# Sixteen conditioning chunks summed on VectorE and POOL, with ones-column products on TensorE, and called at other places

## The chip, the cores and the metric

The kernel runs on one core of a Trainium2 chip. The metric is the device time of one execution in microseconds (us), read as the median of several runs. Engines are named as in the profile: PE is TensorE (its weight loads are PEld), DVE is VectorE, ACT is ScalarE, POOL is GpSimd, SP is SyncE, which issues the loads.

## What is computed

The program is the forward pass of two transformer blocks in float32 on 512 tokens of width 1024. The change lies in the first block. Its conditioning vector `mx` is a product of one row with a 1024 x 6144 matrix:

```python
mx = (jax.nn.silu(c) @ w_ada[l] + b_ada[l])[:, None, :]
sh1, sc1, ga1, sh2, sc2, ga2 = jnp.split(mx, 6, axis=-1)
mc = jax.nn.silu(c_ctx) @ w_ada[l] + b_ada[l]
csh1, csc1, cga1, csh2, csc2, cga2 = jnp.split(mc, 6, axis=-1)
px = modulate(rmsnorm(x, g_norm1[l]), sh1, sc1) @ w_in[l]
x = x + ga1 * branch_merge(px, h_mx, w_fourier[l], w_mlstm[l], w_out[l])
hx2 = modulate(rmsnorm(x, g_norm2[l]), sh2, sc2)
x = x + ga2 * expert_choice(hx2, w_router[l], w_gate_e[l], w_up_e[l], w_down_e[l])
```

Of `mc`, only the first two parts are needed. Between the first and the second modulation stand the projections, a 3x3 grid convolution of q and k, a bidirectional m-LSTM, a Fourier branch and the product with `w_out`.

## The kernel before, in words

`w_ada` is worked off in 24 chunks of 256 columns. `ada_load` (L325) brings one chunk as a raw tile of 128 partitions x 8 x 256, 1 MB, by SP. `ada_sums` (L328) multiplies it on PE: for each k of 0 to 7 the stationary operand is `csil[:, k]`, 128 x 32 (column 0 is silu(c), column 1 silu(c_ctx), the rest zeros), and the moving operand the 256 columns of the chunk. Four k share one bank as four groups of 32 rows. A float32 product runs in two passes, so eight products are 16 rows of the trace. ACT copies the result to `R` (L335), and a product with `sel2`, a 128 x 2 selector, sums the four groups.

The first eight chunks are needed at the start of the block, before anything else, and are not touched. The other sixteen are put into a queue `self.bg`: chunks 12 to 19 by `ada_col` (shift and scale of the second modulation, wanted as columns: `R` is stationary, `sel2` moves; L572), then 8 to 11 and 20 to 23 by `ada_row` (the two gates, wanted as rows: `sel2` is stationary, `R` moves; L559), whose rows go through DRAM (`gad`). Each call of `pump()` (L121) takes one from the queue. It is called where a 1 MB weight tile has just been asked for: in `gemm_ws` (L146), `gemm_ta` (L173), `branch_steps` (L201) and by the k part of the q/k loop (L644). So the sixteen are worked off one by one between 100 and 440 us: four in the q/k convolution stage, two in the Fourier input product, four in the Fourier branch, two in the output gate product, four in the m-LSTM branch.

A weight tile is split before its use by `wsplit` (L125): ACT rounds it to `wH` (L129), POOL subtracts to get `wL` (L130), and PE makes three products for each k (L89, L90, L91; the last one reads `wL`). The q/k convolution (`ev_qk`, L592) is nine taps of multiply and add on DVE (L597, L608); `ctx_state` (L612) does the same for the context (`kacc`, L618 to L622). In the m-LSTM (L664 on), which alternates with the Fourier branch (`branch_steps`, made a generator `fill`), POOL scales `qd` (L682) and adds the two directions (`hs`, L730), which PE then transposes (`hT`, L735). The order on an engine is that of a scheduler, which goes by the dependencies of the program. Loads go into raw tiles that rotate, six of 1 MB at this point.

Of the kernel before, what the change touches and what calls it, by code (L numbers as in the profile page):

```python
# [8 lines left out]
F32 = mybir.dt.float32  # L9
# [3 lines left out]
OP = mybir.AluOpType  # L13
# [68 lines left out]
class Builder:  # L82
# [62 lines left out]

    def gemm_ws(self, w, c0, ncols, act, evac, ct0=0):  # L146

        for cc in range(0, ncols, 256):
            r = self.cols_chunk(w, c0 + cc, 8, 256)
            self.pump()  # L150
            for q in (0, 128):
                evac(ct0 + (cc + q) // 128, self.ws_tile(r, q, act, 8))
# [46 lines left out]
    def branch_steps(self, wb, w_in, gate_off, act, hact, new_th, evac):  # L199

        nc = self.nc  # L201
        for cc in range(0, 1024, 512):
            wr = self.raw(wb[:, cc:cc + 512].rearrange("(k p) c -> p k c", p=128), 4, 512)
            for c2 in range(0, 512, 256):
                gr = self.cols_chunk(w_in, gate_off + cc + c2, 8, 256)
                self.pump()
                for c3 in (0, 128):
                    pg = self.ws_tile(gr, c3, hact, 8)
                    th = new_th()
                    nc.scalar.activation(out=th, in_=pg, func=AF.Tanh, scale=0.5)  # L210
                    py = self.ws_tile(wr, c2 + c3, act, 4)
                    evac((cc + c2 + c3) // 128, th, py)
                    yield
# [105 lines left out]

    def ada_chunk(self, j, pool):  # L320

        return self.ada_sums(self.ada_load(j), pool)

    def ada_load(self, j):
        return self.cols_chunk(self.I["w_ada"][0], j * 256, 8, 256)  # L325

    def ada_sums(self, r, pool):
        nc = self.nc  # L328
        ps = self.pa(256, name="pada")
        for kk in range(0, 8, 4):  # L330
            for q in range(4):
                nc.tensor.matmul(ps[32 * q:32 * q + 32, :], self.csil[:, kk + q, :], r[:, kk + q, :],
                                 start=kk == 0, stop=kk == 4, tile_position=(0, 32 * q))
        R = pool.tile([128, 256], F32, tag="R", name="R")
        nc.scalar.activation(out=R, in_=ps, func=AF.Copy)  # L335
        return R

    def phase_a(self, right):
        tc, nc, I = self.tc, self.nc, self.I
# [216 lines left out]

        self.gad = gad = self.drp.tile([2, 1024], F32, name="gad")

        def ada_row(j):  # L559
            w, c = divmod(j - 8 if j < 12 else j - 16, 4)  # L560
            b = tw(n=256, name="bada")[0:1]
            nc.sync.dma_start(out=b, in_=I["b_ada"][0:1, j * 256:(j + 1) * 256])
            R = self.ada_chunk(j, sm)
            ps = self.pa(256)
            nc.tensor.matmul(ps[0:2], self.sel2, R, start=True, stop=True)
            V.tensor_tensor(b, ps[0:1], b, op=OP.add)
# [5 lines left out]
        def ada_col(j):  # L572
            R = self.ada_chunk(j, sm)
            ps = self.pa(4)
            for q in range(2):
                nc.tensor.matmul(ps[:, 2 * q:2 * q + 2], R[:, q * 128:(q + 1) * 128], self.sel2, start=True, stop=True)
            dst = (self.sh2, self.gs2)[(j - 12) // 4]
            k = 2 * (j % 4)
            c = 112 + 2 * (j - 12)
            pv = ps.rearrange("p (a b) -> p a b", b=2)[:, :, 0]  # L580
            V.tensor_tensor(dst[:, k:k + 2], pv, b1[:, c:c + 2], op=OP.add)
            if j >= 16:
# [58 lines left out]
        for c2 in (0, 256):  # L641
            self.gemm_ws(w_in, OQ + c2, 256, hx, ev_qk, c2 // 128)
            r = self.cols_chunk(w_in, OK_ + c2, 8, 256)
            self.pump()  # L644
            for q in (0, 128):
# [1436 lines left out]
```

## Time and profile before

| what | value |
|---|---|
| median of the runs | 1710.59 us (1710.18 to 1715.16, three runs) |
| the profiled execution | 1714.91 us; its span, first to last instruction, 1713.1 us |
| mean granted clock of PE | 0.969 |
| PE busy | 1579.9 us, 92% of the span |
| DVE busy | 856.2 us, 50% |
| ACT busy | 613.5 us, 36% |
| POOL busy | 564.9 us, 33% |

Durations in the rows below are from the one profiled execution. A busy share is a mean over stages that differ; the stretch that matters here is the first quarter of the span, 80 to 460 us. In a row of a timeline stand the start in us, the busy us, the engine, the line of the program, the operation, the tiles (out<-in), the shapes and how many instructions the row holds; in brackets follow idle time ahead of it and what ended it.

### The profile page before, as it was taken

The page shows a single profiled execution, that of the slowest core. Times are in us where ns is not written, and L with a number is a line of the kernel's source. Part 1 is how long each engine was busy: PE and PEld are TensorE (multiplying, and loading weights), DVE is VectorE, ACT ScalarE, POOL GpSimd, SP SyncE. Part 2 cuts the span into 40 slices and gives each one's busy share as a digit, 9 for nine tenths or more (in the row PEclk, how much of TensorE's full clock was granted, in tenths as well). Part 3 has the DMA queues.
Part 4 walks back from the last instruction along what each step waited for, and adds up shares of the span by engine and source line. Part 5 has one row for each costly group of instructions (what it writes and reads, how often), then busy time and mean ns, then how long its engine had stood idle before and what let it go on. Part 6 is the DMA issues. An engine that isn't in the chain of part 4 may idle for free. (4 is left out here: it accounts for less than half of the span.)

```text
span 1713.1 us, 20867 instructions
## 1 busy us (share of the span) xinstructions
PE 1579.9 (92%) x7702; PEld 1049.7 (61%) x7702; DVE 856.2 (50%) x1595; ACT 613.5 (36%) x1277; POOL 564.9 (33%) x447
## 2 busy tenths in 40 slices
PE   5988999999999999999999978999999989789994
PEld 3766667777776444344344337778666766566663
DVE  4388554423554122022202137997754463667776
ACT  3433354433432000000000034325763354467773
POOL 1213314344513000000000014575443342647765
PEclk9999999999999999999999988999999999889997
DMA  9522412364746999999999983322112328369944
GB/s 302 172 89 91 139 56 93 126 202 148 256 164 245 396 409 409 409 409 409 409 409 409 409 268 124 99 81 91 50 50 85 124 79 327 108 238 346 346 161 165
DMA packets 165548, 381.23 MB, mean 223 GB/s; under 512 B 16302, under 2 KB 74742, under 8 KB 165436
## 3 DMA queue, kind: packets, MB, share of 16 engines
q1 hardware_dynamic: 161116, 371.63, 59.0%
q0 software_dynamic: 4320, 8.16, 1.3%
q8 instruction: 63, 1.03, 0.3%
q14 instruction: 49, 0.40, 0.1%
HBM read 367.40 MB, written 19.93 MB: 226 GB/s over the span
## 5 line engine op out<-in xcount | busy, mean ns | idle before, releaser
L130 POOL TENSOR_TENSOR wL<-raw,wH 128x512 fp32r<-128x512 f32 x220 | 312.0, 1423 | 424.5 <-ACT wH L129 396.1
L129 ACT ACTIVATE wH<-raw 128x512 fp32r<-128x512 f32 x240 | 149.6, 628 | 256.8 <-PE ps L90 149.7
L1068 PE MATMUL ps<-raw,xT 128*64 128x512 f32 x1024 | 240.8, 595 | 0.0
L1068 PEld LDWEIGHTS ps<-raw,xT 128*64 128x64 f32 x1024 | 74.3, 137 | 137.3 <-issue 133.4
L1125 POOL TENSOR_TENSOR yL<-y,yH 128x512 fp32r<-128x512 f32 x14 | 17.9, 1278 | 419.4 <-ACT yH L1124 409.2
L1122 DVE SCALAR_TENSOR_TENSOR y<-ps,valF,ga 128x512 f32<-128x512 f32 x16 | 12.0, 751 | 228.0 <-PE ps L1068 206.8
L91 PE MATMUL ps<-raw,wL 128*128 128x512 f32 (+1 forms) x320 | 120.6, 377 | 2.9 <-POOL wL L130 2.9
L89 PE MATMUL ps<-raw,wH 128*128 128x512 f32 (+1 forms) x320 | 121.3, 379 | 0.7 <-ACT raw L188 0.7
L90 PE MATMUL ps<-raw,wH 128*128 128x512 f32 (+1 forms) x320 | 121.0, 378 | 0.0
L1316 DVE SCALAR_TENSOR_TENSOR cacc<-upad,dwc,cacc 128x512 f32<-128x512 f32 x120 | 118.0, 1036 | 0.9
L1068 PE MATMUL ps<-raw,hidT 128*64 128x512 f32 x448 | 109.3, 594 | 2.8 <-DMA raw<-in_w_down_e 2.8
L89 PE MATMUL ps<-hx,wH 128*128 128x512 f32 x224 | 91.7, 409 | 3.3 <-ACT wH L129 3.3
L91 PE MATMUL ps<-hx,wL 128*128 128x512 f32 x224 | 90.7, 405 | 2.1 <-POOL wL L130 2.1
L1882 DVE TENSOR_TENSOR wL<-raw,wH 128x512 fp32r<-128x512 f32 x96 | 88.4, 976 | 4.6 <-ACT wH L1881 3.3
L1902 POOL TENSOR_TENSOR dL<-raw,dH 128x512 fp32r<-128x512 f32 x64 | 81.6, 1295 | 27.8 <-ACT dH L1901 27.3
L90 PE MATMUL ps<-hx,wH 128*128 128x512 f32 x224 | 90.5, 404 | 0.0
L1124 ACT ACTIVATE yH<-y 128x512 fp32r<-128x512 f32 x16 | 10.0, 626 | 212.7 <-DVE y L1122 212.7
L1107 ACT ACTIVATE hidT<-pa 128x512 f32<-128x512 f32 x16 | 9.6, 597 | 205.0 <-PE pa L1106 205.0
L1068 PEld LDWEIGHTS ps<-raw,hidT 128*64 128x64 f32 x448 | 36.2, 137 | 73.5 <-issue 62.7
L91 PEld LDWEIGHTS ps<-raw,wL 128*128 128x128 f32 x320 | 61.2, 191 | 15.0 <-POOL wL L130 3.4
L89 PEld LDWEIGHTS ps<-raw,wH 128*128 128x128 f32 x320 | 61.4, 192 | 12.2 <-ACT raw L188 1.1
L90 PEld LDWEIGHTS ps<-raw,wH 128*128 128x128 f32 x320 | 61.1, 191 | 11.4 <-issue 0.5
(618 smaller groups left out, 3419.6 us busy)
## 6 DMA issues: line engine op xcount, KB each, us to landing
raw<-in_w_gate_e SPq DMA_DIRECT2D x64, 1024.0 KB
raw<-in_w_up_e SPq DMA_DIRECT2D x64, 1024.0 KB
raw<-in_w_down_e SPq DMA_DIRECT2D x64, 1024.0 KB
raw<-in_w_in SPq DMA_DIRECT2D x34, 1024.0 KB
raw<-in_w_ada SPq DMA_DIRECT2D x24, 1024.0 KB
raw<-in_expert_w_gate SPq DMA_DIRECT2D x32, 512.0 KB
raw<-in_expert_w_up SPq DMA_DIRECT2D x32, 512.0 KB
raw<-in_expert_w_down SPq DMA_DIRECT2D x16, 1024.0 KB
```

The source lines that it names most:

```text
L89: mm(ps, l[0], r[0], start=first, stop=False)
L90: mm(ps, l[0], r[1], start=False, stop=False)
L91: mm(ps, l[1], r[0], start=False, stop=last)
L129: i = self.nc.scalar.activation(out=H, in_=raw_ap, func=AF.Copy)
L130: j = (eng or self.lsub).tensor_tensor(out=L, in0=raw_ap, in1=H, op=OP.subtract)
L1068: nc.tensor.matmul(ps[o, :], act[:, k, o], r[:, q, h * 512:(h + 1) * 512], start=k == 0, stop=k == 7, tile_position=(0, 64 * i))
L1122: V.scalar_tensor_tensor(y, py[e], self.valF[:, p:p + 1], ga2[:, e, :], op0=OP.mult, op1=OP.mult)
L1124: AC.activation(out=H, in_=y, func=AF.Copy)
L1125: (nc.gpsimd if p < 7 else V).tensor_tensor(out=L, in0=y, in1=H, op=OP.subtract)
L1316: V.scalar_tensor_tensor(acc, src, c, acc, op0=OP.mult, op1=OP.add)
L1882: V.tensor_tensor(out=L3, in0=w, in1=H3, op=OP.subtract)
L1902: (nc.gpsimd, V)[DL[i]].tensor_tensor(out=L, in0=src, in1=H, op=OP.subtract)
```

## The change

A new helper `ada_parts` sums a chunk ahead of PE. DVE makes A, 128 x 256, from k = 0 to 4 (one tensor_scalar, four scalar_tensor_tensor, each with one column of `csil` as the scalar). POOL multiplies the three slices k = 5 to 7 in place in the raw tile by their columns of `csil`, broadcast along the row, in one 128 x 768 instruction, and adds the three in two more of 128 x 256. PE then sums over the partitions with a ones column: in `ada_row` two products (ones stationary, A and B moving), in `ada_col` four (A and B stationary in halves of 128 columns, the ones moving). The copy to `R` and the products with `sel2` go away for these sixteen chunks. The second change is where the queue is pumped: `gemm_ws` for q and the k part no longer do it, and `branch_steps` does it for each tile of 128 columns instead of for every two.

```diff
-    def gemm_ws(self, w, c0, ncols, act, evac, ct0=0):
+    def gemm_ws(self, w, c0, ncols, act, evac, ct0=0, pump=True):
...
-            self.pump()
+            if pump:
+                self.pump()
...
                 gr = self.cols_chunk(w_in, gate_off + cc + c2, 8, 256)
-                self.pump()
                 for c3 in (0, 128):
+                    self.pump()
...
+    def ada_parts(self, r, pool):
+
+        V, G = self.nc.vector, self.nc.gpsimd
+        A = pool.tile([128, 256], F32, tag="R", name="A")
+        V.tensor_scalar(A, r[:, 0, :], self.csil[:, 0, 0:1], None, op0=OP.mult)
+        for k in range(1, 5):
+            V.scalar_tensor_tensor(A, r[:, k, :], self.csil[:, k, 0:1], A, op0=OP.mult, op1=OP.add)
+        B = r[:, 5:8, :]
+        G.tensor_tensor(out=B, in0=B, in1=self.csil[:, 5:8, 0:1].to_broadcast([128, 3, 256]), op=OP.mult)
+        for i in (1, 2):
+            G.tensor_tensor(out=B[:, 0], in0=B[:, 0], in1=B[:, i], op=OP.add)
+        return A, B[:, 0]
...
+        ones = sm.tile([128, 1], F32, name="ones", bufs=1)
+        nc.gpsimd.memset(ones, 1.0)
...
-            R = self.ada_chunk(j, sm)
+            AB = self.ada_parts(self.ada_load(j), sm)
             ps = self.pa(256)
-            nc.tensor.matmul(ps[0:2], self.sel2, R, start=True, stop=True)
+            for i, A in enumerate(AB):
+                nc.tensor.matmul(ps[0:1], ones, A, start=i == 0, stop=i == 1)
...
-            R = self.ada_chunk(j, sm)
-            ps = self.pa(4)
+            AB = self.ada_parts(self.ada_load(j), sm)
+            ps = self.pa(2)
             for q in range(2):
-                nc.tensor.matmul(ps[:, 2 * q:2 * q + 2], R[:, q * 128:(q + 1) * 128], self.sel2, start=True, stop=True)
+                for i, A in enumerate(AB):
+                    nc.tensor.matmul(ps[:, q:q + 1], A[:, q * 128:(q + 1) * 128], ones, start=i == 0, stop=i == 1)
...
-            V.tensor_tensor(dst[:, k:k + 2], pv, b1[:, c:c + 2], op=OP.add)
+            V.tensor_tensor(dst[:, k:k + 2], ps, b1[:, c:c + 2], op=OP.add)
...
-            self.gemm_ws(w_in, OQ + c2, 256, hx, ev_qk, c2 // 128)
+            self.gemm_ws(w_in, OQ + c2, 256, hx, ev_qk, c2 // 128, False)
             r = self.cols_chunk(w_in, OK_ + c2, 8, 256)
-            self.pump()
```

The pump places are now: none in the q/k convolution, two in the Fourier input product, eight in the Fourier branch, two in the output gate product, and the first four tiles of the m-LSTM branch. The lines of the changed kernel are 13 or 14 further down: L608 becomes L622, L682 becomes L695, L730 becomes L743.

How this moves instructions is shown at three places. First POOL in the Fourier branch, around the second m-LSTM head; `wL` is the split of a weight tile, `W` the scaling of `qd`, `hs` the addition of the two directions. Before:

```order
L682 TENSOR_TENSOR W<-W,qacc 128x512
L130 TENSOR_TENSOR wL<-raw,wH 128x512 x3
L730 TENSOR_TENSOR hs<-hs,hb 128x256 x2
L682 TENSOR_TENSOR W<-W,qacc 128x512
L130 TENSOR_TENSOR wL<-raw,wH 128x512 x3
```

In the changed kernel, at the same place:

```order
L695 TENSOR_TENSOR W<-W,qacc 128x512
L130 TENSOR_TENSOR wL<-raw,wH 128x512 x3
L344 TENSOR_TENSOR raw<-raw,csil 128x768
L346 TENSOR_TENSOR raw<-raw 128x256 x2
L743 TENSOR_TENSOR hs<-hs,hb 128x256 x2
L695 TENSOR_TENSOR W<-W,qacc 128x512
L130 TENSOR_TENSOR wL<-raw,wH 128x512
L344 TENSOR_TENSOR raw<-raw,csil 128x768
L130 TENSOR_TENSOR wL<-raw,wH 128x512
L346 TENSOR_TENSOR raw<-raw 128x256 x2
L130 TENSOR_TENSOR wL<-raw,wH 128x512
```

A multiply and its two adds now stand ahead of the two `hs`, and a multiply and its adds around the next `wL`.

Second DVE in the q/k convolution, at the second k tile; `qacc` is a sum of taps, `kacc` that of the context. Before:

```order
L597 TENSOR_SCALAR qacc<-qin,cols_85 128x512
L608 SCALAR_TENSOR_TENSOR qacc<-qin,cols_85,qacc 128x7x63 x2
L608 SCALAR_TENSOR_TENSOR qacc<-qin,cols_85,qacc 128x448
L610 SCALAR_TENSOR_TENSOR qacc<-qin,qacc 128x512
L608 SCALAR_TENSOR_TENSOR qacc<-qin,cols_85,qacc 128x7x63
L618 TENSOR_SCALAR kacc<-kin,cols_85 128x256
L608 SCALAR_TENSOR_TENSOR qacc<-qin,cols_85,qacc 128x8x63
```

In the changed kernel:

```order
L611 TENSOR_SCALAR qacc<-qin,cols_85 128x512
L340 TENSOR_SCALAR A<-raw,csil 128x256
L622 SCALAR_TENSOR_TENSOR qacc<-qin,cols_85,qacc 128x7x63
L624 SCALAR_TENSOR_TENSOR qacc<-qin,qacc 128x512
L622 SCALAR_TENSOR_TENSOR qacc<-qin,cols_85,qacc 128x448
L342 SCALAR_TENSOR_TENSOR A<-raw,csil,A 128x256
L622 SCALAR_TENSOR_TENSOR qacc<-qin,cols_85,qacc 128x7x63
L632 TENSOR_SCALAR kacc<-kin,cols_85 128x256
L622 SCALAR_TENSOR_TENSOR qacc<-qin,cols_85,qacc 128x8x63
```

One chain for A is woven in between the taps; its last three links follow a few rows later.

Third PE at a row chunk of the Fourier branch; `hT` is the transposition of `hs`, the rows of L89 to L91 with `hx` are the gate product. Before:

```order
L735 MATMUL hT<-ident,hs 128x128 x4
L678 MATMUL bcM<-MS,selR 128x512
L332 MATMUL pada<-raw,csil 32x256 x8
L90 MATMUL ps<-hx,wH 128x512
L91 MATMUL ps<-hx,wL 128x512
L89 MATMUL ps<-hx,wH 128x512
L565 MATMUL pa<-R,sel_81 2x256
```

In the changed kernel:

```order
L748 MATMUL hT<-ident,hs 128x128 x4
L691 MATMUL bcM<-MS,selR 128x512
L579 MATMUL pa<-A,ones 1x256
L579 MATMUL pa<-raw,ones 1x256
L90 MATMUL ps<-hx,wH 128x512
L91 MATMUL ps<-hx,wL 128x512
L89 MATMUL ps<-hx,wH 128x512
```

The eight csil products and the product with the selector have given way to two products with the ones column.

## Rows read from the trace of the kernel before

**Rows 1.** Busy us (instructions) by stretch: PE, PEld, DVE, ACT, POOL; granted clock, DMA share, GB/s.

```profile
107.00:190.00 83.00, 72.50 (x388) 55.55 (x386) 71.44 (x109) 26.59 (x55) 25.27 (x17) 0.90 0.32 101
...
240.00:270.00 30.00, 29.63 (x165) 23.12 (x164) 13.78 (x36) 15.40 (x38) 11.32 (x10) 1.00 0.23 76
...
415.00:440.00 25.00, 25.00 (x129) 17.78 (x128) 9.57 (x11) 8.59 (x15) 9.63 (x8) 1.00 0.52 176
```

**Rows 2.** Waits of PE in the convolution, 107 to 190 us: total, times, longest.

```profile
PE pa L625 <- DVE kacc L622: 5.4, 4, 2.0
PE ps L89 <- ACT wH L129: 3.0, 1, 3.0
PE ps L91 <- POOL wL L130: 1.7, 3, 1.0
```

**Rows 3.** Waits of PE from 240 to 460 us, all of them.

```profile
PE hT L735 <- POOL hs L730: 1.5, 4, 0.4
PE ps L91 <- POOL wL L130: 0.4, 1, 0.4
```

**Rows 4.** Timeline of PE at a row chunk and at a column chunk.

```profile
434.07 1.07 PE L332 MATMUL pada<-raw,csil 128*32 128x256 f32 x16
435.07 0.50 PE L89 MATMUL ps<-hx,wH 128*128 128x512 f32 x1
435.41 0.40 PE L90 MATMUL ps<-hx,wH 128*128 128x512 f32 x1
435.64 0.39 PE L91 MATMUL ps<-hx,wL 128*128 128x512 f32 x1
435.96 0.59 PE L565 MATMUL pa<-R,sel 128*2 128x256 f32 x2
436.49 0.51 PE L89 MATMUL ps<-hx,wH 128*128 128x512 f32 x1
...
269.82 0.50 PE L576 MATMUL pa<-sel,R 128*128 128x2 f32 x4
270.18 0.48 PE L90 MATMUL ps<-hx,wH 128*128 128x512 f32 x1
```

**Rows 5.** The tile kacc: ns min/median/max, first and last start.

```profile
L618 DVE TENSOR_SCALAR kacc<-kin,cols x4: 341/344/349, 125.7 to 182.6; 128x256 f32<-128x256 f32 x4
...
L622 DVE SCALAR_TENSOR_TENSOR kacc<-kth,kacc x4: 408/412/417, 128.6 to 188.4; 128x256 f32<-128x256 f32 x4
```

**Rows 6.** Timelines of DVE and POOL: taps alone, taps beside L761, and L761.

```profile
115.70 3.75 DVE L608 SCALAR_TENSOR_TENSOR qacc<-qin,cols,qacc 128x441 f32<-128x441 f32 x6
...
160.00 8.74 DVE L608 SCALAR_TENSOR_TENSOR qacc<-qin,cols,qacc 128x448 f32<-128x448 f32 x7
...
163.29 4.98 POOL L761 TENSOR_TENSOR dL<-raw,dH 128x512 fp32r<-128x512 f32 x3
```

**Rows 7.** Timeline of DVE at the longest wait for a chunk.

```profile
149.74 0.16 DVE L581 TENSOR_TENSOR sh<-pa,cols 128x2 f32<-128x2 f32 x1 [3.97 <-PE pa L576]
```

**Rows 8.** Timelines of POOL and PE in the m-LSTM branch: two splits, a first reader.

```profile
404.87 1.29 POOL L130 TENSOR_TENSOR wL<-raw,wH 128x512 fp32r<-128x512 f32 x1 [1.50 <-ACT wH L129]
407.65 1.29 POOL L130 TENSOR_TENSOR wL<-raw,wH 128x512 fp32r<-128x512 f32 x1 [1.48 <-ACT wH L129]
...
410.18 0.39 PE L91 MATMUL ps<-hx,wL 128*128 128x512 f32 x1
```

**Rows 9.** Timelines of POOL and PE in the Fourier branch, at the second direction's end.

```profile
292.25 1.27 POOL L130 TENSOR_TENSOR wL<-raw,wH 128x512 fp32r<-128x512 f32 x1 [1.10 <-ACT wH L129]
294.35 0.73 POOL L730 TENSOR_TENSOR hs<-hs,hb 128x256 f32<-128x256 f32 x1 [0.82 <-DVE hb L729]
296.02 0.73 POOL L730 TENSOR_TENSOR hs<-hs,hb 128x256 f32<-128x256 f32 x1 [0.94 <-DVE hb L729]
...
296.81 0.65 PE L735 MATMUL hT<-ident,hs 128*128 128x128 f32 x4 [0.36 <-POOL hs L730]
```

**Rows 10.** Busy time by stretch, columns as in the first group, at a pause of PE.

```profile
102.00:106.00 4.00, 0.26 (x2) 0.28 (x3) 3.91 (x4) 1.62 (x3) 1.26 (x1) 0.62 0.05 13
106.00:110.00 4.00, 4.00 (x15) 3.48 (x15) 3.01 (x6) 2.02 (x4) 0.23 (x1) 0.52 0.06 16
```

More of the change, by code (lines that the diff above doesn't have):

```diff
@@ L318, in consts2 @@
         self.dw = load_cols([(I["conv_dw_w_2"][0].rearrange("w (k p) -> (w k) p", p=128), 124)], 124, "dwc")
-    def ada_chunk(self, j, pool):
-        return self.ada_sums(self.ada_load(j), pool)
     def ada_load(self, j):
@@ L579, in ada_col @@
             c = 112 + 2 * (j - 12)
-            pv = ps.rearrange("p (a b) -> p a b", b=2)[:, :, 0]
-            V.tensor_tensor(dst[:, k:k + 2], pv, b1[:, c:c + 2], op=OP.add)
+            V.tensor_tensor(dst[:, k:k + 2], ps, b1[:, c:c + 2], op=OP.add)
             if j >= 16:
```

## The prediction

> **What bounds the kernel now.** I read first the table by stretches, then the waits of TensorE in those stretches, then single rows. The change acts between about 80 and 460 us of the span; behind that, every engine has the same instructions in the same order, so whatever shift has built up by 460 us passes through to the end. Two stages have different limits [rows 1]. From 107 to 190 us, the q/k convolution, VectorE (DVE) is busy 71.44 of 83 us and TensorE (PE) 72.50, at a granted clock of 0.90: neither is full, they wait for each other. From 240 us on PE is the bound: 29.63 of 30 us, later 25.00 of 25, at clock 1.00, with DVE and POOL each under half. The waits say the same: in the convolution PE waits 5.4 us for DVE's `kacc`, 3.0 for a split on ScalarE (ACT) and 1.7 for POOL's `wL` [rows 2]; from 240 to 460 us it waits 1.5 us for POOL's `hs` and 0.4 for `wL`, and for nothing else [rows 3]. So a microsecond taken from PE after 240 us counts in full if nothing else comes late, and a microsecond given to DVE in the convolution counts nearly in full.
>
> **PE: removed and added.** A row chunk costs PE its eight csil products, 434.07 to 435.07, 1.00 us, and the sel2 product, 435.96 to 436.49, 0.53 us [rows 4]. Each switch between kinds of product adds some 0.1 us: the first L89 behind them lasts 0.34 us to its successor, the next 0.23 [rows 4]. With about four such switches that is 1.9 us a row chunk. A column chunk has 1.00 and 0.36 (269.82 to 270.18) [rows 4] and the switches: 1.6 to 1.7. Afterwards a row chunk is two ones products of the form of the one sel2 product, 2 x 0.53 and the switches, 1.2; a column chunk is four products with a 128x128 stationary operand and one moving column, twice what the 0.36 us were, 0.72, and the switches, 0.8. Of the sixteen chunks four columns stood in the convolution; four columns and eight rows (12 chunks) stood behind it, where PE bounds: 4 x 1.6 + 8 x 1.9 = 21.6 us. Now all sixteen stand behind it, 8 x 0.8 + 8 x 1.2 = 16.0. **Term 1: -5.6 us** (-4 to -8, as the unknown switches go). The four columns' 6.4 us leave the convolution as well, but there DVE is the limit; that belongs to term 2.
>
> **DVE and POOL: the unit costs.** The chain A is one 128x256 tensor_scalar and four 128x256 scalar_tensor_tensor; `kacc` has both shapes, 0.344 and 0.412 us [rows 5]: 0.34 + 4 x 0.41 = 2.0 us a chunk. On POOL a 128x512 takes 1.29 us [rows 8] and a 128x256 0.73 [rows 9]; on the line through both a 128x768 is 1.85. With the two adds a group is 1.85 + 2 x 0.73 = 3.3 us. Its multiply reads a broadcast operand that no row of before has; the ends are 2.2 us in all (three equal 128x256) and 4.3, if each operation is stretched as the three L761 were, 4.98 / 3 = 1.66 instead of 1.29 [rows 6]. I take 3.3, nearest to the undisturbed rows. Sixteen chunks are 32 us of DVE and 53 us of POOL; both have the room on average, so the place decides.
>
> **The convolution.** Of the chains only one lies wholly among the q/k taps (it stands in the order rows of DVE above); one is done earlier and two later, in idle time: +2.0 us. Two POOL groups run beside the taps. What that costs is in the rows: six taps alone took 3.75 us, 0.63 each; seven beside L761 took 8.74 instead of 4.4, so DVE lost 4.3 us in 4.98 us of POOL, 0.87 for each [rows 6]. Two groups of 3.3 us, with DVE busy 0.86 of the time [rows 1], cost about 2 x 3.3 x 0.87 x 0.86 = 5.0. Against it DVE no longer sits 3.97 us ahead of L581 until PE has done a chunk's L576 [rows 7], nor runs that L581 of 0.16: -4.1. **Term 2: +2.0 + 5.0 - 4.1 = +2.9 us.** Its ends: no collision at all and a little less PE work in the way, -3; the wait of 3.97 us replaced by another for PE, +6.
>
> The Trainium skill has a harsher rule (SBUF — State Buffer, section "SBUF: two separate sides"): a VectorE operation with two SBUF inputs and a GpSimd operation exclude each other for the whole instruction, they don't share. By it the 5.0 us would be 6.6 and the sum 1.6 us more. The trace agrees nearly: 0.87 lost of each microsecond, not 1.
>
> **POOL in the PE-bound stages.** POOL takes its instructions in order, so a group delays what is queued behind it, `wL` or `hs`, which PE waits for. Between one `wL` and the next POOL idles 1.49 us, and a `wL` that ends at 408.94 (407.65 + 1.29) is first read at 410.18, 1.24 us later [rows 8]. A group of 3.3 us in such a gap makes the next `wL` 3.3 - 1.49 - 1.24 = 0.56 us late, one of 4.3 us 1.6. By the order four groups sit in gaps of just this kind: one in the Fourier input product, one in the Fourier branch, two in the m-LSTM branch. That is 2.2 to 6.4 us; I take 3.3, with one of the four stretched (3 x 0.56 + 1.6). One group sits directly ahead of the two `hs` additions. There `wL` ends at 293.52, the first `hs` starts at 294.35 and the second ends at 296.75 [rows 9]; with the group between, they can't start before 296.8 and end at 298.3, 1.5 us late, and PE's `hT` already waited 0.36 us [rows 9], so all of it shows; 2.5 if stretched, and I take 1.7. The other groups have gaps of 4 to 8 us. **Term 3: +5.0 us** (+2 to +10). It is a new kind of wait: PE behind POOL.
>
> Costed at nothing: the sixteen ACT copies and their evictions, since ACT is under half busy where PE is the bound; the loads, the same 16 from the same queue, some issued later because the raw tile is now read by POOL, which the six rotating tiles cover (if not, a product waits for a load, as PE never does after 240 us [rows 3]); and the moved calls, whose row results are needed far behind the last chunk.
>
> **The sum.** -5.6 + 2.9 + 5.0 = +2.3 us on the profiled execution's 1714.91 us, 1717.2. That execution lies 4.3 us above the median of the three runs, 1710.59; the same shift on the median gives 1712.9, so **1713 us**. A measurement of this kernel tells about 0.3% (5 us) from no change, so this reads as no change.
>
> **Rivals.**
> - *The saving comes through.* Groups of POOL go into its idle time as the averages suggest, and DVE's lost 3.97 us of waiting pays for the chain. For it: POOL idles longer than a group in most places, and its multiply may be quicker than the line. Against it: the two places above, where the order leaves no room. Term 3 is 1, term 2 is -3: -7.6, **1703 us**, faster.
> - *POOL becomes the late engine.* Its price is that of rows 6 and 8 together: groups stretched to 4.3 us by DVE's chains, so 4 x 1.6 + 2.5 = 8.9 us. It decides from a group length of 2.7 us (1.49 + 1.24); at 3.3 each place costs half a microsecond, at 4.3 three times that. Longer pauses also cost clock: from 102 to 106 us PE was busy 0.26 of 4 us, and the next 4 us were granted 0.52 [rows 10], nearly the lower of the two levels (1.2 GHz), about 2 us lost. With one such loss: -5.6 + 2.9 + 10.9 = +8.2, **1719 us**, slower. Against it: most groups have room, and a clock of 1.00 has held over pauses of 0.4 us.
> - *The convolution is lost to DVE.* The idle 3.97 us return as a wait for `qin` or PE, and DVE stands still for the whole of both groups, 2 x 3.3 = 6.6: term 2 is 2.0 + 6.6 = 8.6. -5.6 + 8.6 + 5.0 = +8.0, **1719 us**, slower. For it: DVE has under 12 us of slack in 83. Against: PE has 6.4 us less to do there. The page of the skill named above states this exclusion.
> - That the change doesn't do what it says has no weight: the order shows the csil products of the sixteen chunks gone and all sixteen calls moved.
>
> **How the numbers follow.** The forecast, between 1706 and 1716, has 0.42; the saving that comes through 0.27; POOL late 0.18; the lost convolution 0.13. So faster 0.27, same 0.42, slower 0.31. The likeliest case itself spans 1706 to 1716; cases of both signs hold more than half, so the range reaches to both: 1702 to 1722, which leaves out a saving with no stall at all and both slow rivals together.
>
> **What would show it.** Right: PE's busy time about 12 us lower; L332 a third of its former count; from 240 to 460 us waits of PE for `wL` and `hs` of 4 to 6 us instead of 1.9, the largest at one `hT`; the convolution's end (the last L610's successor) 2 to 4 us later; POOL's groups 3.3 us, 53 us in all. Wrong: no waits for POOL after 240 us (then faster), the clock below 1.00 there, or taps that take as long as now beside the groups. Above all it is wrong if PE idles in the convolution for something not named, for 6.4 us of its work leave that stage.

## The result: 1733.38 us, slower by 1.27%, and the profile after

The changed kernel took 1733.38 us (median of four runs, 1731.6 to 1736.69); the kernel before, on the same chip, 1712.88 (1710.18 to 1716.1). The ratio is 1.0127, with a 95% interval of 1.0109 to 1.0144: 20.5 us slower, above the upper end of the range. The profiled executions differ by less, a span of 1729.7 against 1713.1 us, since that of before lay 2.0 us above this median and that of after 1.8 below its own: 16.6 + 2.0 + 1.8 = 20.4. Trace differences below are to be read against the 16.6.

The first part of the page after, to be held against the table of before:

```profile
PE 1569.8 (91%) x7494; PEld 1047.2 (61%) x7494; DVE 921.5 (53%) x1675; ACT 606.5 (35%) x1261; POOL 623.1 (36%) x496
```

PE has 10.1 us less to do, DVE 65 and POOL 58 us more. PE alone is near full, at 91%; 10 us less work there went with 17 us more time.

The same table by stretches as [rows 1], with five stretches of the Fourier branch, the output gate product and the m-LSTM branch added:

```profile
107.00:190.00 83.00, 66.55 (x327) 52.83 (x326) 78.54 (x112) 26.32 (x54) 36.56 (x24) 0.94 0.18 58
240.00:270.00 30.00, 28.84 (x156) 23.03 (x155) 20.53 (x46) 13.89 (x32) 16.89 (x15) 1.00 0.37 123
270.00:300.00 30.00, 26.46 (x144) 21.08 (x143) 17.39 (x40) 12.81 (x30) 16.48 (x15) 0.98 0.38 124
300.00:345.00 45.00, 42.29 (x217) 32.66 (x216) 31.80 (x63) 19.13 (x46) 22.61 (x20) 0.98 0.37 123
345.00:375.00 30.00, 25.90 (x117) 19.84 (x115) 10.46 (x15) 6.23 (x12) 14.62 (x13) 0.89 0.66 225
375.00:395.00 20.00, 18.57 (x77) 12.76 (x76) 12.38 (x16) 5.44 (x10) 13.48 (x11) 1.00 0.51 168
395.00:415.00 20.00, 17.12 (x65) 11.20 (x64) 13.83 (x24) 5.80 (x10) 12.35 (x13) 0.91 0.46 144
415.00:440.00 25.00, 25.00 (x107) 19.19 (x106) 9.31 (x11) 9.87 (x17) 13.01 (x11) 1.00 0.56 200
```

Between 300 and 415 us PE is now idle for 11.1 us and its granted clock is 0.89 and 0.91 in two stretches; before, the same 115 us had 0.73 us of idling and a clock of 1.00 throughout. Neither POOL nor DVE is busy for more than 0.71 of any of these four stretches: the loss is one of lateness, not of load.

Where it came, by events of both traces (the start in before, then the shift): the last row of `u` in the Fourier input product 209.79, -6.3 us; first `hT` 267.21, -3.4; second 296.81, +0.2; fourth 352.88, +8.6; last `sO` of the output gate product 379.14, +16.9; first `oL` behind the m-LSTM branch 457.38, +12.9; end of the span, +16.6. So the convolution with the Fourier input product gained 6 us; up to the first `hT` 3 were lost, from there to the fourth 12, in the output gate product 8; the m-LSTM branch gave back 4, and 3.7 came behind `oL`. Of the 8, 5.4 arose on DVE: ACT's copy of the same `sO`, directly behind PE, is 11.5 us later (378.52 and 390.05).

The waits of PE from 260 to 480 us, as in [rows 3]:

```profile
PE hT L748 <- POOL hs L743: 8.3, 4, 4.1
PE ps L89 <- ACT wH L129: 3.8, 3, 2.1
PE ps L91 <- POOL wL L130: 2.5, 3, 1.1
```

Together 14.6 us against 1.9 before. The largest are two of the four `hT`. The second, with what stands ahead of it, in the timelines of POOL and PE (compare [rows 9]):

```profile
292.50 1.48 POOL L344 TENSOR_TENSOR raw<-raw,csil 128x768 f32<-128x768 f32 x1 [1.58 <-DMA raw<-in_w_ada]
294.05 1.52 POOL L346 TENSOR_TENSOR raw<-raw 128x256 f32<-128x256 f32 x2
295.53 1.40 POOL L743 TENSOR_TENSOR hs<-hs,hb 128x256 f32<-128x256 f32 x2
...
296.99 0.66 PE L748 MATMUL hT<-ident,hs 128*128 128x128 f32 x4 [3.15 <-POOL hs L743]
```

The group is the predicted one, 1.48 + 1.52 = 3.0 us here, ahead of both `hs`, and POOL also stands at its head until the chunk has landed. PE waits 3.15 us, where 1.5 more than the 0.36 of before were forecast.

The fourth, in the timelines of POOL, DVE and PE, with two slices of the table behind it:

```profile
353.66 1.47 POOL L344 TENSOR_TENSOR raw<-raw,csil 128x768 f32<-128x768 f32 x1 [1.96 <-DMA raw<-in_w_ada]
355.09 1.33 POOL L130 TENSOR_TENSOR wL<-raw,wH 128x512 fp32r<-128x512 f32 x1
356.39 1.91 POOL L346 TENSOR_TENSOR raw<-raw 128x256 f32<-128x256 f32 x2
359.00 0.89 POOL L743 TENSOR_TENSOR hs<-hs,hb 128x256 f32<-128x256 f32 x1 [0.70 <-DVE hb L742]
360.72 0.72 POOL L743 TENSOR_TENSOR hs<-hs,hb 128x256 f32<-128x256 f32 x1 [0.83 <-DVE hb L742]
...
353.61 1.67 DVE L340 TENSOR_SCALAR A<-raw,csil 128x256 f32<-128x256 f32 x1 [0.18 <-DMA raw<-in_w_ada]
355.31 1.39 DVE L342 SCALAR_TENSOR_TENSOR A<-raw,csil,A 128x256 f32<-128x256 f32 x1
...
358.51 0.41 DVE L742 TENSOR_TENSOR hb<-num,ad 128x256 f32<-128x256 f32 x1
...
361.50 1.11 PE L748 MATMUL hT<-ident,hs 128*128 128x128 f32 x4 [4.10 <-POOL hs L743]
...
355.00:360.00 5.00, 2.40 (x14) 1.74 (x13) 4.93 (x10) 0.17 (x1) 4.11 (x5) 1.00 0.75 253
360.00:365.00 5.00, 3.50 (x10) 1.62 (x11) 0.95 (x3) 0.60 (x1) 0.72 (x1) 0.50 0.00 0
```

One landing of a chunk releases the chain and the group within 0.05 us of each other, and each is then in the way of the other. The `tensor_scalar` of the chain ends just behind POOL's multiply, 1.67 us instead of 0.344 [rows 5]; the next step ends just behind POOL's `wL`, 1.39 instead of 0.412; `hb`, queued among the chain's steps, comes at 358.51 although PE ended its last `num` product at 355.78 (355.39 + 0.39); so `hs` is late by both queues. What ends last is DVE's: the second `hs`, at 360.72, again waits for its `hb`. PE waits 4.10 us and is then granted 0.50, the lower of its two levels, over the next slice.

The third place is the output gate product, in timelines of DVE, ACT and PE:

```profile
378.11 2.48 DVE L340 TENSOR_SCALAR A<-raw,csil 128x256 f32<-128x256 f32 x2 [4.10 <-DMA raw<-in_w_ada]
380.51 0.68 DVE L827 SCALAR_TENSOR_TENSOR sO<-sO,hd 128x512 f32<-128x512 f32 x1
...
381.23 0.64 ACT L192 ACTIVATE hmH<-sO 128x512 fp32r<-128x512 f32 x1 [4.94 <-DVE sO L827]
397.34 0.63 ACT L192 ACTIVATE hmH<-sO 128x512 fp32r<-128x512 f32 x1 [6.71 <-DVE sO L827]
...
398.54 0.50 PE L89 MATMUL ps<-hmH,wH 128*128 128x512 f32 x1 [2.12 <-ACT wH L129]
```

DVE stood for a chunk's load and then did two first steps of chains, and behind them waited `sO`, which ACT splits for the m-LSTM branch. The last `sO` shows how this reaches PE: ACT waits 6.71 us for it, the next `wH` stands behind it in ACT's queue, and PE waits 2.12 us for that `wH`.

The costs of chains and groups, from the groups of instructions between 60 and 480 us (count, busy us, mean ns, idle time ahead):

```profile
L342 DVE SCALAR_TENSOR_TENSOR A<-raw,csil,A 128x256 f32<-128x256 f32 x64 | 44.2, 707 | 0.6
L346 POOL TENSOR_TENSOR raw<-raw 128x256 f32<-128x256 f32 x32 | 27.6, 862 | 2.0
L344 POOL TENSOR_TENSOR raw<-raw,csil 128x768 f32<-128x768 f32 x16 | 25.2, 1572 | 23.6 <-DMA raw<-in_w_ada 23.6
L340 DVE TENSOR_SCALAR A<-raw,csil 128x256 f32<-128x256 f32 x16 | 14.7, 929 | 30.2 <-DMA raw<-in_w_ada 12.3 <-PE pa L591 11.8 <-PE ps L91 3.8
```

A group is (25.2 + 27.6) / 16 = 3.3 us, as forecast; a chain (44.2 + 14.7) / 16 = 3.7 instead of 2.0. And POOL waits 23.6 us for loads at the head of groups.

### The profile page after: what moved, and what is told of

Read it like the earlier page. It is cut to its first block, busy times and chain, and to the rows that moved or that the text cites. A ratio compares the mean times of both kernels' runs of the same rounds, so it can differ in the third digit from the quotient of the medians.

```text
span 1729.7 us, 20570 instructions
## 1 busy us (share of the span) xinstructions
PE 1569.8 (91%) x7494; PEld 1047.2 (61%) x7494; DVE 921.5 (53%) x1675; ACT 606.5 (35%) x1261; POOL 623.1 (36%) x496
## 5 line engine op out<-in xcount | busy, mean ns | idle before, releaser
L130 POOL TENSOR_TENSOR wL<-raw,wH 128x512 fp32r<-128x512 f32 x220 | 317.1, 1448 | 372.3 <-ACT wH L129 342.4
L91 PE MATMUL ps<-raw,wL 128*128 128x512 f32 (+1 forms) x320 | 120.5, 377 | 2.9 <-POOL wL L130 2.9
L89 PE MATMUL ps<-raw,wH 128*128 128x512 f32 (+1 forms) x320 | 121.7, 380 | 0.7 <-ACT raw L189 0.7
L89 PE MATMUL ps<-hx,wH 128*128 128x512 f32 x224 | 92.6, 413 | 5.2 <-ACT wH L129 5.2
L91 PE MATMUL ps<-hx,wL 128*128 128x512 f32 x224 | 91.9, 410 | 5.2 <-POOL wL L130 5.1
L91 PEld LDWEIGHTS ps<-raw,wL 128*128 128x128 f32 x320 | 61.2, 191 | 15.1 <-POOL wL L130 3.4
L89 PEld LDWEIGHTS ps<-raw,wH 128*128 128x128 f32 x320 | 61.3, 192 | 12.3 <-ACT raw L189 1.1
L90 PEld LDWEIGHTS ps<-raw,wH 128*128 128x128 f32 x320 | 61.3, 192 | 11.5 <-issue 0.5
```

Of the source, the lines that this page charges most:

```text
L89: mm(ps, l[0], r[0], start=first, stop=False)
L90: mm(ps, l[0], r[1], start=False, stop=False)
L91: mm(ps, l[1], r[0], start=False, stop=last)
L130: j = (eng or self.lsub).tensor_tensor(out=L, in0=raw_ap, in1=H, op=OP.subtract)
```

## The experiments

Four causes were held against each other: the **length of POOL's group** ahead of `wL` and `hs`; the **exclusion** of chain and group, which stretches both; the **waits for the chunk's load** at the head of POOL's and DVE's queues; and the **new places** of the calls. In the diffs, minus is the changed kernel unless said otherwise; e1 and so on are short names.

**Sums and places apart.** e1 keeps the new sums at the old places; e2 the old products on PE at the new places.

```diff
e1: gemm_ws(w_in, OQ + c2, ...) and the k part pump again; branch_steps pumps once per c2
-                for c3 in (0, 128):
-                    self.pump()
+                self.pump()
+                for c3 in (0, 128):
e2:
-            AB = self.ada_parts(self.ada_load(j), sm)
+            R = self.ada_sums(self.ada_load(j), sm)
(and the products with sel2 as before)
```

> The sums on DVE and POOL as in the changed kernel, but the queue is pumped at the old places (four chunks in the q/k convolution, one per two tiles in the Fourier branch). Theory W (the chain and the multiply stand in their queues and wait for the chunk's load, and what PE needs waits behind them): with one chunk per two tiles the raw tiles turn over more slowly and loads are in time more often, so about half of the 20 us come back: 1718 to 1724. Theory L (DVE and POOL work on one chunk lasts too long beside each other, whatever the load does): four groups leave the PE-bound stages, but DVE's convolution gets four chains: 1728 to 1735. Theory P (the new places alone are at fault): as before or better, 1704 to 1713.

Measured: 1736.22 us, ratio 1.0152 (1.0124 to 1.0179).

> The sums on PE as before the change (csil products, R, sel2), but at the new places: none in the convolution, one per branch tile. Theories W and L: no chain and no multiply is there to block a queue; the convolution gains about 6 us as it did in the changed kernel and four chunks of 1.6 us come back behind it: 1709 to 1715, as before. Theory P: as slow as the changed kernel, 1728 to 1735.

Measured: 1714.74 us, ratio 1.0018 (1.0005 to 1.0031). The places alone are worth almost nothing over the whole: up to `u` they gain 7.1 us, and by the fourth `hT` they are 1.4 behind, since the Fourier branch now has eight chunks where it had four. The new sums lose at either set of places. The cause is in the sums.

**The two halves of the sums.** e4 cuts both (one `tensor_scalar` on DVE, one 128x256 multiply on POOL), e8 cuts POOL's half alone, e9 DVE's alone; these three leave out terms of the sums, while loads, products and places stay. e5 does all eight terms on DVE, nothing on POOL, and has one ones product where the change has two.

```diff
e4 (e9 has the first edit alone, e8 the second):
-        for k in range(1, 5):
+        for k in range(1, 1):
...
-        B = r[:, 5:8, :]
+        B = r[:, 5:6, :]
...
-        for i in (1, 2):
+        for i in ():
e5:
-        for k in range(1, 5):
+        for k in range(1, 8):
-        B = r[:, 5:8, :]
...
-        return A, B[:, 0]
+        return A,
```

> The changed kernel with the work per chunk cut to one tensor_scalar on DVE and one 128x256 multiply on POOL (the terms k = 1 to 4, 6 and 7 are left out, so the conditioning values of these sixteen chunks are wrong); loads, products and places stay. Theory W: the two instructions still wait for the load at the head of their queues: 1722 to 1732. Theory L: the work is gone, so 1706 to 1714. Theory P: 1728 to 1735.

Measured: 1707.83 us, ratio 0.9979 (0.9962 to 0.9995).

> All eight terms of a chunk summed on DVE (one tensor_scalar, seven scalar_tensor_tensor, 3.2 us by the undisturbed rows), nothing on POOL, half the ones products. Theory D (DVE's queue costs: the chain stands ahead of additions, products and splits that PE waits for): the chain is longer, so as slow as the changed kernel or worse, 1728 to 1738. Theory G (POOL's queue costs: the group stands ahead of wL and hs): gone, 1706 to 1714. Theory M (chain and group start at the same landing and exclude each other, and so each is nearly twice as long): the chain takes 3.2 us instead of 3.7 and POOL is free, 1714 to 1724.

Measured: 1699.08 us, ratio 0.9918 (0.9901 to 0.9935): **faster than both kernels**, by 12.5 us than before (1711.62 beside it) and by 34 than the change.

> The changed kernel with the whole chain on DVE, and on POOL only one 128x256 multiply (the terms k = 6 and 7 are left out of the sums). Theory D: 1726 to 1733. Theory G: 1706 to 1713. Theory M: the chain falls to about 2.6 us, 1712 to 1718.

Measured: 1711.16 us, ratio 1.0001 (0.9986 to 1.0017).

> The changed kernel with only the tensor_scalar on DVE (the terms k = 1 to 4 are left out of the sums), and the whole group on POOL. Theory D: 1706 to 1713. Theory G: 1726 to 1733. Theory M: the group keeps its 3.3 us without a partner, 1712 to 1718.

Measured: 1725.95 us, ratio 1.0078 (1.0061 to 1.0096).

From e4 the rest of the chain costs 3.3 us (e8), the rest of the group 18.1 (e9), and both 25.5 (the change): **POOL's half carries most of the loss**. The 4 us left over for both together are within the uncertainty of four medians, whose ratios have intervals some 0.3% wide, 5 us each. The stage where the change loses, from `u` to `oL`, divides otherwise in the profiled executions: 245.0 us in e4, 248.6 in e8, 253.6 in e9, 266.8 in the change, so 3.7 for the chain, 8.6 for the group and 9.5 only where both are there; e9 is another 6.0 later than e4 ahead of `u`. The group is the larger part by either count; how much comes only from the two together is not settled. e5 is shown by the groups of instructions and the table by stretches:

```profile
L342 DVE SCALAR_TENSOR_TENSOR A<-raw,csil,A 128x256 f32<-128x256 f32 x112 | 78.9, 720 | 1.5
L340 DVE TENSOR_SCALAR A<-raw,csil 128x256 f32<-128x256 f32 x16 | 8.7, 552 | 8.0 <-DMA raw<-in_w_ada 8.0
```

```profile
300.00:345.00 45.00, 44.64 (x244) 36.06 (x244) 34.38 (x75) 18.39 (x45) 19.34 (x16) 1.00 0.55 189
345.00:375.00 30.00, 29.60 (x126) 21.70 (x125) 18.74 (x33) 10.32 (x18) 12.42 (x11) 1.00 0.61 196
375.00:395.00 20.00, 20.00 (x85) 14.88 (x84) 15.32 (x25) 7.14 (x12) 9.84 (x8) 1.00 0.68 219
395.00:415.00 20.00, 19.47 (x84) 14.85 (x83) 7.28 (x9) 7.71 (x14) 12.15 (x9) 1.00 0.39 133
```

A chain is now (78.9 + 8.7) / 16 = 5.5 us, longer than in the change, and yet PE is idle for 1.3 us between 300 and 415 us at a clock of 1.00. By the durations of [rows 4], half of the ones products, 0.36 us in each of eight column chunks and 0.5 in each of eight row chunks, are 6.9 us of PE's work that e5 does not have. Of e5's lead of 12 us over e8, the profiled executions show 4.5 ahead of `oL` (443.85 and 448.39) and 5.2 behind it, where e8 has a wait in the router that e5 has not (below); against the change these are 26.4 and 5.0.

**The places again, with e5's sums.** e14 is e5 at the old places (e1's edit of the places).

> All eight terms on DVE, but pumped at the old places: four chains in the convolution, where DVE was busy 71 of 83 us. Each has 3.2 us, 13 us in all, and the stage has 12 us of slack that is not all usable: 1706 to 1716, slower than the same sums at the new places (1699) by 7 to 17 us. If the places don't matter: 1697 to 1702.

Measured: 1713.26 us, ratio 1.0007 (0.9997 to 1.0018). With the sums on DVE the new places are worth 14 us: in the convolution, where DVE is the limit, e14 had PE wait 9.0 us for a chain.

**The waits for the load.** e3 issues a chunk's load one call earlier and sums the one before; e6 is e3 with e5's sums; e18 leaves the load where it is and does the sums behind the weight tile's products.

```diff
e3, in pump:
-        if self.bg:
-            self.bg.pop(0)()
+        work, self.pend = self.pend, None
+        if self.bg:
+            j, f = self.bg.pop(0)
+            r = self.ada_load(j)
+            self.pend = lambda: f(j, r)
+        if work:
+            work()
...
e18: the last two lines are a pump2(), called behind the products of the weight tile
```

> The changed kernel, but each call loads the next chunk and sums the one loaded at the call before, so the load has one branch tile more to land. Theory W: POOL's 23.6 us of waiting for the chunk's load nearly vanish, and with them most of the loss: 1712 to 1720. Theory L: the same work at nearly the same places, 1728 to 1735. Theory P: 1728 to 1735.

Measured: 1729.0 us, ratio 1.0099 (1.0072 to 1.0126).

> All eight terms on DVE, and each call loads the next chunk and sums the one loaded at the call before. In the run without this, DVE waited 8 us for chunks; if these waits hold up what PE needs: 1692 to 1697; if they fall where DVE is idle: 1697 to 1702.

Measured: 1700.55 us, ratio 0.994 (0.9924 to 0.9957), no gain over e5.

> The load of a chunk is issued where it is, but its sums (chain, group and products) come only behind the products of the weight tile it was issued beside: POOL has that tile's wL ahead of the group, and the chunk lies in the tile long before. Work, instructions and shapes are those of the change. If the loss is the wait for the chunk's load at the head of POOL's queue (17.9 us in the rows of the change), it is gone: POOL's waits for loads before L344 fall below 3 us and the time falls to some 1712 to 1718 (the change less 15 to 20). If the loss is the group's own length in a gap too short for it, with chain and group excluding each other, it stays, since each group still has a next wL or hs behind it: 1728 to 1738, with the waits for loads gone all the same.

Measured: 1729.02 us, ratio 1.0106 (1.0077 to 1.0135).

Neither e3 nor e18 took the waits away, so neither is the clean test it was meant to be: POOL still waited 32.9 us for chunks in e3 and 15.2 in e18. But the runs together answer it. The row of POOL's wait in e3, and then in e4:

```profile
POOL raw L349 <- DMA raw<-in_w_ada: 32.9, 9, 6.1
```

```profile
POOL raw L344 <- DMA raw<-in_w_ada: 29.3, 11, 5.5
```

POOL's waits and the medians, in pairs: 7.1 us and 1736.22 (e1), 15.2 and 1729.02 (e18), 23.6 and 1733.38 (the change), 25.9 and 1725.95 (e9), 27.1 and 1711.16 (e8), 29.3 and 1707.83 (e4), 32.9 and 1729.0 (e3). The longest waits but one belong to the fastest of these kernels, the shortest to the slowest; and among the four that do the full sums (e1, e18, the change, e3) the time does not rise with the wait. In sum, these waits are not what costs; at single places, as at 353.66, they make a group later.

**Chain and group one after the other.** e10 has POOL's multiply read a copy of its factors that DVE makes from the finished chain, so they cannot run at once.

```diff
+        cb = pool.tile([128, 3, 1], F32, tag="cb", name="cb", bufs=2)
+        V.tensor_scalar(cb, self.csil[:, 5:8, 0:1], A[:, 0:1], A[:, 0:1], op0=OP.add, op1=OP.subtract)
...
-        G.tensor_tensor(out=B, in0=B, in1=self.csil[:, 5:8, 0:1].to_broadcast([128, 3, 256]), op=OP.mult)
+        G.tensor_tensor(out=B, in0=B, in1=cb.to_broadcast([128, 3, 256]), op=OP.mult)
```

> The changed kernel, but POOL's multiply takes its three columns from a copy that DVE writes when the chain is done, so chain and group of one chunk never run together. Theory D: the chain falls from 3.7 to about 2.1 us, and with it about half of the loss: 1718 to 1726. Theory G: the group is later by the chain, so POOL's queue blocks longer: 1732 to 1742. Theory M: both run at their undisturbed length: 1714 to 1722.

Measured: 1724.8 us, ratio 1.0073 (1.0051 to 1.0096). Chains shrink to (37.7 + 6.9) / 16 = 2.8 us, and some 9 us come back, 8.6 by the medians and 8.8 between `u` and `oL` of the traces. The collision of a chain with its own group is part of the loss; that part may be larger than 9 us, since e10 also puts the group later.

**Idle groups beside e5.** To price POOL's work by itself, e5 was given POOL work whose results nobody uses: e11 four 128x256 operations per chunk, e12 the same with the first reading the chunk, e13 nine memsets of 128x256.

```diff
e11, against e5 (e12: in0=r[:, 7, :]; e13: nine G.memset(B, 0.0); csil stands for its flat view):
+        B = pool.tile([128, 256], F32, tag="R", name="B")
+        G.tensor_tensor(out=B, in0=csil, in1=csil, op=OP.mult)
+        for i in range(3):
+            G.tensor_tensor(out=B, in0=B, in1=csil, op=OP.add)
```

> The kernel that sums all eight terms on DVE, with an idle group added on POOL per chunk: four 128x256 operations on a tile of its own, about 2.9 us, with inputs that are always there; nothing uses the result. Theory W (POOL's queue stands still until the chunk has landed): no load to wait for, 1699 to 1703. Theory N (the group's own length stands ahead of wL and hs): 1706 to 1716. Theory X (POOL's group and DVE's operations with two inputs exclude each other, so that DVE is late): 1706 to 1716.

Measured: 1728.8 us, ratio 1.0102 (1.0085 to 1.0119).

> The same with one input changed: the group's first operation reads the chunk's raw tile, so that it waits for the load; order and lengths stay. Theory W: 1710 to 1722. Theories N and X: as the run without the load, within 3 us.

Measured: 1734.39 us, ratio 1.0124 (1.0105 to 1.0142).

> The idle group without a load to wait for, made of nine 128x256 memsets, about 2.8 us, that read nothing. Theory X: nothing is read, so no exclusion, 1699 to 1703. Theory N: as the run with four operations, 1706 to 1716. Theory W: 1699 to 1703.

Measured: 1716.4 us, ratio 1.0025 (1.0012 to 1.0038). These three have a flaw: B shares the two buffers of A, so that chains waited 22.8, 24.8 and 7.7 us for POOL to free one. They were made anew with a tile of their own: e15 nine 128x64 operations, e16 the same with the first reading the chunk, e17 one such operation and 14 memsets. In e15 and e17 the first operation reads the weight tile beside which the chunk is asked for, which holds the group to its place.

```diff
e15, against e5 (e16: in0=r[:, 7, 0:64]; e17: 14 G.memset(self.Bs, 0.0) for the loop):
+        G.tensor_tensor(out=self.Bs, in0=self.tie, in1=c64, op=OP.mult)
+        for i in range(8):
+            G.tensor_tensor(out=self.Bs, in0=self.Bs, in1=c64, op=OP.add)
```

> All eight terms on DVE, and an idle group on POOL per chunk: nine 128x64 operations, about 2.8 us, on a tile that nothing else uses, so that DVE never waits for it. Its first operation reads the weight tile that the next product needs anyway, not the chunk. Theory N (length in POOL's queue): 1704 to 1712. Theory X (exclusion of DVE by POOL's reads): 1704 to 1712. Theory W (waiting for the chunk's load): 1699 to 1702. If the tile shared with DVE's sums made the earlier idle groups slow: 1699 to 1704.

Measured: 1734.88 us, ratio 1.0139 (1.0122 to 1.0156).

> The same idle group, but its first operation reads the chunk's raw tile and so waits for its load. Theory W: 5 to 15 us more than the run that reads the weight tile. Theories N and X: within 3 us of it.

Measured: 1729.02 us, ratio 1.0103 (1.0087 to 1.012).

> The same idle group, reading the weight tile first and then fourteen 128x64 memsets that read nothing, of about the same length. Theory X: 1699 to 1702, since only reads exclude DVE. Theory N: as the run with nine operations, within 3 us.

Measured: 1709.28 us, ratio 0.9991 (0.9982 to 1.0001).

No theory on record had e5 so fast or the idle groups so dear: e11, e12 and e15 lie 12 to 23 us above the highest of their ranges, and e16 and e17 fit none.

The idle group of e15 brings back the whole loss: 36 us over e5, with DVE's chains as e5 has them. Its waits of PE between 260 and 480 us, and then its groups of instructions:

```profile
PE ps L91 <- POOL wL L130: 15.7, 8, 4.9
PE hT L754 <- POOL hs L749: 6.1, 4, 5.0
```

```profile
L351 POOL TENSOR_TENSOR Bs<-Bs,csil 128x64 f32<-128x64 f32 x128 | 50.1, 392 | 9.3
...
L349 POOL TENSOR_TENSOR Bs<-raw,csil 128x64 f32<-128x64 f32 x16 | 8.8, 548 | 18.3 <-DMA raw<-in_w_in 17.6
```

The same two views of e17:

```profile
PE ps L91 <- POOL wL L130: 8.5, 7, 2.0
...
PE hT L752 <- POOL hs L747: 1.2, 3, 0.5
```

```profile
L349 POOL MEMSET Bs<- 128x64 f32 x224 | 34.7, 155 | 12.0
L347 POOL TENSOR_TENSOR Bs<-raw,csil 128x64 f32<-128x64 f32 x16 | 8.7, 546 | 19.4 <-DMA raw<-in_w_in 18.7
```

A group of (50.1 + 8.8) / 16 = 3.7 us costs 36 us; one of (34.7 + 8.7) / 16 = 2.7 us, nearly all memsets, costs 10. (The window leaves out e17's first `hT`, at 259.00, which waited 2.97 us.) Neither waits for the chunk, and e16, which does, is no slower than e15. Both wait at the head of the group for the weight tile, 17.6 us in e15 and 18.7 in e17, so that wait is not what sets them apart. So POOL work between splits is enough to cause the loss. How, the largest wait of e15 shows, in the timelines of POOL and PE:

```profile
262.70 3.10 POOL L351 TENSOR_TENSOR Bs<-Bs,csil 128x64 f32<-128x64 f32 x8
...
266.27 1.11 POOL L351 TENSOR_TENSOR Bs<-Bs,csil 128x64 f32<-128x64 f32 x3
267.35 0.72 POOL L749 TENSOR_TENSOR hs<-hs,hb 128x256 f32<-128x256 f32 x1
...
268.12 1.11 PE L754 MATMUL hT<-ident,hs 128*128 128x128 f32 x4 [4.96 <-POOL hs L749]
```

One group and the first operations of the next stand without a pause ahead of `hs`, whose `hb` was done at 262.65 (262.23 + 0.42).

Two things separate e15 from e17, a microsecond of length and that the operations read SBUF. The Trainium skill (SBUF — State Buffer, section "SBUF: two separate sides") says that a VectorE operation with two SBUF inputs is locked out only against a GpSimd operation that reads SBUF. The trace of e17 agrees: ten steps of chains that ran beside memsets and nothing else of POOL's took 471 to 485 ns, as long as the 46 beside an idle POOL (477 on the mean), while the 43 beside its other operations alone, `wL` above all, took 996. But e15's short additions did not hold the chains up either: eleven steps beside them alone took 489 ns on the mean. What grew there was the group itself, whose additions took 0.32 us beside an idle DVE and 0.50 beside a busy one. So the loss of e15 is not one of late chains; it lies in what stands in POOL's queue.

## Why the prediction was wrong, by its own steps

**Term 1, PE: right.** PE's busy time fell by 10.1 us (forecast about 12), although products at the lower clock last longer; e4 and e8, with the same products, have 14.0 and 19.0 less than before.

**Term 2, the convolution: wrong sign.** +2.9 us were forecast; by the prediction's own mark, the start of the last `qacc` step of L610 (L624 after), the convolution gained 7.6 (193.44 and 185.81), and with the Fourier input product 6.3. The price of the collisions was half the forecast: 64 taps, eight first and eight last steps of `qacc` took 53.9 + 4.8 + 6.8 = 65.5 us before and 56.5 + 6.0 + 5.5 = 68.0 after, 2.5 us more where 5.0 stood. And the step "the four columns' 6.4 us leave the convolution as well, but there DVE is the limit", which gave them no worth beyond one wait of 3.97 us, failed: e2, which moves them and leaves the sums on PE, gains 7.1 us up to `u`. The change gains 0.8 less than e2 there; that is what its sums cost in these two stages, net of what they save PE.

**Term 3, POOL in the PE-bound stages: the term that failed.** +5.0 us were forecast, at most 10. From `u` to `oL` the change lost 12.9 + 6.3 = 19.2 us, e2 at the same places 1.8 + 7.1 = 8.9, although the change has some 10 us less for PE there (term 1's 0.8 and 0.7 us in each of the 14 chunks behind `u`); so the sums cost about 10 + 10 = 20 us in waits and clock. The change against e4, which has the same products and the sums cut short, says 21.8 over the same stretch. The prediction's own sign, 4 to 6 us of waits for `wL` and `hs`, came out at 10.8 (8.3 + 2.5). Of the step's parts:

- The group's length, 3.3 us, was right.
- "Four groups sit in gaps of just this kind ... The other groups have gaps of 4 to 8 us" was not. It read the gaps from a trace in which every landing, split and `hb` stood where the old order had put it. With chunks landing as they do, groups fell into other gaps: the fourth `hT`, which had no term, waited 4.10 us.
- The chain behind 240 us was costed at nothing on DVE's mean load. It is released by the same landing as the group, the two run beside each other, and `hb` and `sO` are queued in it: 3.7 us a chain. e10 gives 9 us back by parting them; e8 shows that the chain without a full group costs little, 3.3 us.
- The output gate product had no term at all, and lost 8 us: `sO` behind chains, and behind `sO` the `wH` that PE waits for; `wL` behind groups.
- The clock was left to a rival at one loss of 2 us. Between 270 and 415 us the table's granted clocks give 30 x 0.02 + 45 x 0.02 + 30 x 0.11 + 20 x 0.09 = 6.6 us at most (where PE idles, a low clock costs nothing), beside 14.7 us of idling in the same stretches (before: 1.1, at 1.00).

**Not in any term: 3.5 us at 1500 us of the span**, in the second block's router, where every engine has the same instructions in the same order. One row of before and then three of after, all from timelines:

```profile
1490.26 0.17 DVE L1747 TENSOR_SCALAR s<-s 128x8 f32<-128x8 f32 x1
```

```profile
1504.26 4.64 DVE L1760 TENSOR_SCALAR s<-s 128x8 f32<-128x8 f32 x1
...
1502.27 3.93 POOL L1688 TENSOR_TENSOR hm<-xres,raw 128x512 f32<-128x512 f32 x2
1506.15 2.73 POOL L1847 MEMSET xsb<- 128x1024 f32 x3
```

In the changed kernel DVE first waits 1.27 us for a small load (`in_tri`), and the short operation then falls beside POOL's two `hm` and three memsets and ends 0.02 us behind the last of them (1508.90 and 1508.88), ahead of what PE's `lg` needs: that wait is 7.3 us instead of 1.1. e1, e4, e8, e10 and e18 have it too, and e3 with 7.9; in e2, e5, e14, e15 and e17 it is 1.1, in e9 1.9. So up to 5 us of a difference between two of these kernels can come from here: "whatever shift has built up by 460 us passes through to the end" holds but for such chances.

**The rivals.** "POOL becomes the late engine" had the mechanism, the place and the sign, at 1719 us: its price, 8.9 us for four gaps and one `hs` and 2 us for one loss of clock, was too small by the same step. Its condition, a group stretched beyond 2.7 us, did not need stretching: 3.3 was beyond it already. "The convolution is lost to DVE" was wrong, "the saving comes through" right for the convolution alone.

**What stays open:** how the loss divides between the group's mere length in POOL's queue and its running beside a chain. The wait at 268.12 in e15 is the group's length alone, the one at 361.50 in the change has both. Between `u` and `oL` e10 gives back 8.8 us, and e4, e8 and e9 leave 9.5 to the two together; by the medians it is 4. Places and order of the groups differ a little between all these kernels, so these shares are estimates.

## What to carry to other kernels

Work that is moved from a full engine to an idle one should be costed by what is queued behind it there, not by the idle share: 53 us on a POOL that was a third busy cost some 20, since the splits and additions that PE waits for stood behind it. Try such work on the engine whose queue holds less of what the bound engine reads next (all eight terms on DVE: 1699.08 us, longer chains and a faster kernel), and keep two engines from being released by the same landing (e10: 9 us). A stage in which two engines wait for each other can gain from work taken off the one that looks less like the limit (e2: 7.1 us in the convolution).

## What the runs showed of the hardware that was not expected

- POOL's 128x768 multiply with a broadcast operand took 1.48 us on the median of sixteen (1.47 to 1.92), less than the 1.85 us of the line through 128x256 and 128x512.
- A `tensor_scalar` with one SBUF tensor as input stood beside POOL as the two-input steps do: 1.67 us for 128x256 instead of 0.344, and 4.64 for 128x8 instead of 0.17. The Trainium skill (SBUF — State Buffer, section "SBUF: two separate sides") states it for VectorE operations with two SBUF inputs and for those in a two-port mode; these rows fit the second case, but show no mode. The 128x8 operation also outlasted three memsets, which read nothing.
- POOL's memset of 128x64 took 152 ns on the median in e17, its addition of the same shape 322 in e15; beside a busy DVE the addition took 0.50 us, the memset hardly longer than alone (0.16 on the mean).
